# Delta rule with feature-major outputs: sums of squares by VectorE's 32x32 turns

## The chip, the cores and the metric

The kernel runs on one core of a Trainium2 chip. The metric is the device time of one execution in microseconds. A core has five engines that work through queues of their own and wait for each other by semaphores: TensorE (PE, with its weight loads as PEld), VectorE (DVE), ScalarE (ACT), GpSimd (POOL), and SyncE (SP), which here only issues DMAs. DMAs are also issued from POOL's queue.

## What is computed

A decoder of two layers over 1,024 tokens of 1,024 features. Each layer projects the normed input once, feeds a sparse attention branch and a gated delta rule branch, gates both, adds them and projects the sum back:

```python
for layer in range(DEPTH):
    h = rms_norm(x, norm_gain[layer])
    proj = h @ w_in[layer]
    ...
    y_a = dsa_attention(q_a, k_a, v_a, q_i, k_i, w_i) * jax.nn.silu(z_a)
    qkv_b = jax.nn.silu(causal_depthwise_conv(qkv_b, conv_w[layer]))
    ...
    q_b = l2_normalize(q_b.reshape(B, S, GDN_HEADS, GDN_DK))
    k_b = l2_normalize(k_b.reshape(B, S, GDN_HEADS, GDN_DK))
    ...
    o_b = chunked_gated_delta_rule(q_b, k_b, v_b, beta, g).astype(x.dtype)
    y_b = (rms_norm(o_b, gdn_norm_gain[layer]) * jax.nn.silu(z_b)).reshape(B, S, GDN_WIDTH)
    gates = jax.nn.sigmoid(gate_l).reshape(B, S, N_BRANCH, D_MODEL)
    mixed = gates[:, :, 0, :] * y_a + gates[:, :, 1, :] * y_b
    x = x + mixed @ w_out[layer]
return rms_norm(x, final_gain)
```

The change concerns two normalizations of the delta rule branch, which has eight heads of 128 features: the length of each token's query (`l2_normalize(q_b)`) and the mean square of each token's output (`rms_norm(o_b)`). The delta rule is linear in the query. So the kernel runs it on raw queries and divides once, at the output: with the sum of squares of a raw query Q, and of an unnormalized output O over 128 features, the factor for a token is the inverse root of O/128 + 128 EPS (Q + 4 EPS), apart from constants.

## The kernel before

**Phases.** Each layer has a token phase (index scores and top-k selection beside token-major projections), a feature phase (the delta rule and the remaining gates) and an attention phase with the output projection. The change lies in the feature phase, which runs from about 340 us to 1,000 us in layer 0 and once more from about 1,600 us in layer 1.

**The feature phase.** `feature_phase` goes over the eight heads. For each it projects keys, queries and values (`kf`, `qf`, `vv`, each with 128 features on the partitions and 1,024 tokens in the free dimension) and then two gates of the head before. A projection half is 24 matmuls of 512 columns (L419): eight blocks of 128 input features, three products each, because every f32 operand is split into a high and a low part (`w_hi`, `w_lo`; the split is a cast on ACT, L164, and a subtraction on DVE, L165). A head is 6 halves for kf, qf and vv and 4 for the gates, 240 matmuls in all.

**The order of the work.** All else is hung onto these matmuls. `self.count` counts them, and `plan_head` writes for each step of a head the count at which it is issued (`AT_...`, relative to the head's start; the first head's late steps are 28 later). After each matmul, `planned` issues the steps that are due, with a high priority, and a list scheduler then orders each engine's instructions by what it reckons to be ready. A head's steps spread over more than two of its own lengths of 240, so a stretch of 240 counts holds the late steps of one head, the chunks of the next and the early steps of a third. Below, a count within such a stretch is the count since its kf projection began.

**A head's steps**, in their order:
- `conv` (L847): three DVE passes over 1,024 columns (L866), a tanh on ACT into the buffer `xp` (L868), a last DVE pass (L869).
- `decays_load` (L824): SP loads 512 KB of decay rows into `H`, each row of DRAM read for all 128 partitions (L831); POOL masks it (L832) and then issues the load of `qe`, 512 KB of the same kind (L838).
- `gdn_keys` (100, 106): four PE transposes per half, squares on ACT, a reduce (L885) and the scaled copy `kdec` on DVE (L897), then some ten DVE steps on 8 columns for the keys' lengths (`g_rk` to `g_nce`).
- `gdn_queries` (142, 147): four PE transposes of `qf` per half (L878), squares on ACT (L884), a reduce on DVE (L885); then `zq` (L931).
- `gdn_row` (152): sends the row of key factors through DRAM, `cscr` (L919) to `g_ccomp` (L922), and with `gdn_products` (151 to 163) come the key-key and query-key products. `A` holds the decayed query-key products.
- `gdn_inverse`, `inverse_pairs` (336 to 366, so 96 to 126 of a later stretch): the inverse of a triangular matrix per chunk of 128 tokens. In 32x32 blocks it goes through DRAM and a chain of small DVE steps (L1050, L1052); the pairs are then joined on PE. DVE turns blocks into `xf` (L1069), PE makes L1078, L1085, L1092, then L1098, from which DVE makes `xf` (L1100), which PE uses in L1104.
- `gdn_chunks` (374 on, one step each 7 counts): for eight chunks in turn, the state `st`, the update `u`, and the output `po`. Its products put tokens on the partitions (L996, L997). ACT copies `po` into `vb` and squares it with an accumulated sum per token into `osq` (L998, L1000).
- `gdn_finish` (L1004): the gates of the head (`gate` tiles, 128x512, features on the partitions), then `norms` (537): `ms` from `osq` and `zq`, the inverse root in eleven small DVE steps (`rsqrt`, L147 to L160), the scaling of `vb` (L1015); and `outputs` (546, 552): four PE transposes of `vb` per half (L1021), a product with gain and gate from PSUM on DVE (L1022), a store to `yb` (L1023).

Of the kernel before, what the change touches and what calls it, by code (L numbers as in the profile page):

```python
# [20 lines left out]
try:  # L21
# [4 lines left out]
F32 = mybir.dt.float32  # L26
# [5 lines left out]
OP = mybir.AluOpType  # L32
# [4 lines left out]
P = 128  # L37
# [42 lines left out]
    76, (126, 130, 134, 138), (100, 106), (142, 147), (151, 155, 159, 163), 152, 184, (204, 210))  # L80
AT_SECOND, AT_PAIRS, AT_CHUNKS, AT_NORMS, AT_OUTPUTS = 38, 336, 374, 537, (546, 552)

STEP_PAIRS, STEP_CHUNKS = 6, 7
# [24 lines left out]
class Trunk:  # L108
    def __init__(self, ctx, tc, args):
        self.tc, self.nc = tc, tc.nc  # L110
        (self.x, self.positions, self.norm_gain, self.w_in, self.conv_w, self.a_log, self.dt_bias,
         self.gdn_gain, self.idx_gain, self.w_out, self.final_gain, self.out) = args
        self.depth = self.w_in.shape[0]
        self.const = ctx.enter_context(tc.tile_pool(name="const", bufs=1))
        self.dram = ctx.enter_context(tc.tile_pool(name="scratch", bufs=1, space=DRAM))
        self.small = ctx.enter_context(tc.tile_pool(name="small", bufs=2))
        edge = ctx.enter_context(tc.tile_pool(name="edge", bufs=1)).tile([P, 32], F32, name="edge")
        self.nc.vector.memset(edge, 0.0)
        self.act = ctx.enter_context(tc.tile_pool(name="act", bufs=1))
        self.wp = ctx.enter_context(tc.tile_pool(name="bulk", bufs=1))  # L120
        self.tags, self.turn = {}, 0
        self.beside, self.credit = None, 0.0
        self.ahead, self.scored = {}, False
        self.plan, self.count, self.act_last = [], 0, None
        ctx.enter_context(self.banks(acc=(1, 2), tr=(1, 2)))
# [20 lines left out]

    def rsqrt(self, v, n, y=None):  # L147

        nc = self.nc
        if y is None:  # L150
            y = self.small.tile([P, n], F32, name="rs_y")
        t = self.small.tile([P, n], F32, name="rs_t")
        yi = y.bitcast(I32)
# [27 lines left out]
    def constants(self, first):  # L181
# [25 lines left out]
        for q in range(4):  # L207
            nc.gpsimd.affine_select(self.xinit[32 * q:32 * q + 32], self.xinit[32 * q:32 * q + 32],
                                    pattern=[[4, 8], [-1, 32]], compare_op=OP.not_equal, fill=1.0, base=q,
                                    channel_multiplier=0)  # L210
        self.rope_tables()

        self.feat, self.ig, self.nexpa, self.dtb = [], [], [], []
# [518 lines left out]

    def gated(self, l, ht, cz, cg, tag="acc"):

# [3 lines left out]
        for half in range(2):  # L738
            b = p.tile([P, 512], F32, name="gate", bufs=2)
            for i in range(2):  # L740
# [7 lines left out]

    def gate_a(self, l, ht, f, tag="acc", then=None):

        for _ in self.gate_steps(l, ht, f, tag, then):
            pass

    def gate_steps(self, l, ht, f, tag, then=None):
        for half, b in enumerate(self.gated(l, ht, C_ZA + f * P, C_GA + f * P, tag)):
            self.stored = self.nc.sync.dma_start(out=self.ya[f, :, 512 * half:512 * half + 512], in_=b).ins
# [5 lines left out]
    def feature_phase(self, l, ht):  # L762
# [6 lines left out]
        with tc.tile_pool(name="early", bufs=1) as pe, tc.tile_pool(name="decays", bufs=1) as pd, \  # L769
# [10 lines left out]
            for h in range(HEADS + 1):  # L780
                before, hd = hd, None
                if h < HEADS:
                    hd = dict(h=h, at=self.count)
                    self.plan_head(p, hd, XF)
                    for name, base, bufs in (("kf", 1024, 3), ("qf", 0, 3), ("vv", 2048, 1)):
                        self.conv(l, pe if name == "vv" else p, ht, hd, name, base, bufs)
                if h in GATED:
                    i = 1 + GATED.index(h)
                    for f in range(sum(GATES[:i]), sum(GATES[:i + 1])):
                        self.gate_a(l, ht, f)  # L790
                if before:
# [3 lines left out]
    def plan_head(self, p, hd, XF):  # L795
# [21 lines left out]
        chunks = self.gdn_chunks(p, hd)  # L817
        at(AT_CHUNKS, *[lambda: next(chunks, None)] * (3 * T - 1), gap=STEP_CHUNKS)

    def zeros(self, a):  # L820
# [26 lines left out]
    def conv(self, l, p, ht, hd, name, base, bufs):  # L847
# [22 lines left out]
        if name == "kf":  # L870
            self.behind = done.ins

    def turned(self, src, half):
# [50 lines left out]
    def gdn_queries(self, hd, half):  # L924

        self.squares(self.turned(hd["qf"], half), hd["ssq"][:, 8 + 4 * half:12 + 4 * half])
        if half == 1:


            zq = hd["zq"] = self.small.tile([P, T], F32, name="g_zq")  # L930
            self.nc.vector.tensor_scalar(zq, hd["ssq"][:, 8:16], 4 * EPS, P * EPS, op0=OP.add, op1=OP.mult)  # L931

    def gdn_products(self, p, hd, c):
# [30 lines left out]
    def gdn_chunks(self, p, hd):  # L964
# [3 lines left out]
        egt = self.egt[:, :, h]  # L968
        osq = hd["osq"] = sm.tile([P, T], F32, name="g_osq")
        st = None  # L970
        for c in range(T):
# [14 lines left out]
            if c < T - 1:  # L986
# [5 lines left out]
                else:  # L992
                    nc.vector.scalar_tensor_tensor(new, st, egt[:, c:c + 1], pn, op0=OP.mult, op1=OP.add)
            po = self.bank("oc")[:, :P]
            if st is not None:
                nc.tensor.matmul(po, qf[:, cs], st, start=True, stop=False)  # L996
            nc.tensor.matmul(po, A[:, c], u, start=st is None, stop=True)  # L997
            nc.scalar.copy(vb[:, c], po)  # L998
            junk = self.pl.tile([P, P], F32, name="o_junk", bufs=1)
            nc.scalar.activation(junk, po, AF.Square, accum_out=osq[:, c:c + 1])  # L1000
            st = new
            yield

    def gdn_finish(self, l, p, ht, hd):  # L1004
# [12 lines left out]
        def outputs(half):  # L1017
# [5 lines left out]
            nc.sync.dma_start(out=self.yb[h, :, 512 * half:512 * half + 512], in_=b)  # L1023

        self.at(hd["at"] + AT_NORMS, norms)
        for half in range(2):
# [365 lines left out]
```

## Time and profile before

| | |
|---|---|
| median of 3 runs | 2548.41 us (2547.25 to 2548.49) |
| profiled execution | 2547.07 us, its span 2545.3 us |
| PE busy | 2508.8 us, 99% |
| PEld busy | 2100.8 us, 83% |
| DVE busy | 1875.3 us, 74% |
| ACT busy | 1329.9 us, 52% |
| POOL busy | 207.4 us, 8% |
| granted TensorE clock | 0.995 |
| DMA | 211.35 MB, mean 83 GB/s |

An instruction's row gives its start in us from the span's start, its duration, engine, line, operation, and the tiles written and read (out<-in). Brackets hold the idle time of the engine before it and what ended that. A group's row gives the count, the busy time in us, the mean duration in ns, and idle time before the group's instructions. Matmuls overlap: a record of 0.39 us can be followed by the next after 0.23. What a matmul costs PE is therefore read from the spacing of starts. POOL's and SP's rows of DMAs tell when one is issued, not when it lands.

### The profile page before, as it was taken

To read this page: it belongs to the slowest core of one execution; us is meant where nothing else is said; L and a number is where in the kernel's file an instruction comes from. 1 tells how busy PE (TensorE), PEld (TensorE's weight loads), DVE (VectorE), ACT (ScalarE), POOL (GpSimd) and SP (SyncE) were. 2 spreads that over 40 slices of the span, in tenths; PEclk is the share of its full clock that TensorE was granted. 3 is DMA by queue.
4 is the path that set the end of the run, shared out by engine and by line. 5 is a ranking of instruction groups with operands and counts; after the bars stand their busy time and mean duration, and the time that the engine had idled before them with its cause. 6 is when DMAs were issued, how large, how long until landed. Compare 5 with 4: busy or idle time off the path is not lost.

```text
span 2545.3 us, 42024 instructions
## 1 busy us (share of the span) xinstructions
PE 2508.8 (99%) x14874; PEld 2100.8 (83%) x14874; DVE 1875.3 (74%) x5057; ACT 1329.9 (52%) x3052; POOL 207.4 (8%) x510
## 2 busy tenths in 40 slices
PE   8999999999999999999999999999999999999998
PEld 7778878888888888898897788788888888888986
DVE  7569997777787773797555789877777787638965
ACT  5449943344444342797234598334344444338952
POOL 0234000000000000000202330000000000000010
PEclk9999999999999999999999999999999999999999
DMA  4123243322333331431421232433322222324223
GB/s 129 55 67 102 66 103 77 73 53 70 69 70 75 75 92 60 156 95 33 157 74 52 73 97 71 100 72 71 76 52 68 72 73 69 103 86 133 82 94 126
DMA packets 290807, 211.35 MB, mean 83 GB/s; under 512 B 72290, under 2 KB 252356, under 8 KB 290596
## 3 DMA queue, kind: packets, MB, share of 16 engines
q1 hardware_dynamic: 277876, 167.43, 24.4%
q0 software_dynamic: 12576, 40.97, 5.5%
q8 instruction: 117, 1.92, 0.3%
q14 instruction: 94, 0.77, 0.1%
q10 hardware_dynamic: 144, 0.26, 0.0%
HBM read 162.19 MB, written 46.40 MB: 82 GB/s over the span
## 4 chain that ended last, share of the span: by engine, by line
PE 64%; DVE 20%; issue 7%; ACT 3%; DMA 3%; POOL 2%; SPq 0%; DVEq 0%; ACTq 0%; POOLq 0%
PE acc L419 20%; PE more L419 9%; PE acc L394 8%; PE acc L1257 4%; PE wide L1225 4%; DVE xtmp L1050 3%; DVE t_junk L646 3%; DVE xc L1052 3%; PE tr L1248 2%; PE tr L944 2%; PE out L394 2%; DVE w_lo L165 2%; DVE kf L866 2%; PE tr L878 2%; DMA w_raw<-in_w_in_dram 1%
## 5 line engine op out<-in xcount | busy, mean ns | idle before, releaser
L419 PE MATMUL acc<-hi_t,w_hi 128*128 128x512 f32 x1152 | 468.9, 407 | 7.1 <-ACT th L743 7.1
L419 PE MATMUL acc<-lo_t,w_hi 128*128 128x512 f32 x1152 | 467.2, 406 | 0.0
L419 PE MATMUL acc<-hi_t,w_lo 128*128 128x512 f32 x1152 | 463.4, 402 | 0.0
L164 ACT CAST w_hi<-w_raw 128x512 fp32r<-128x512 f32 (+1 forms) x336 | 200.3, 604 | 301.5 <-PE acc L419 134.3
L165 DVE TENSOR_TENSOR w_lo<-w_raw,w_hi 128x512 fp32r<-128x512 f32 (+1 forms) x336 | 222.5, 670 | 130.2 <-ACT w_hi L164 112.4
L394 PE MATMUL acc<-w_hi,hi_t 128*128 128x512 f32 (+1 forms) x688 | 254.4, 370 | 8.6 <-ACT hi_t L164 7.9
L419 PEld LDWEIGHTS acc<-hi_t,w_hi 128*128 128x128 f32 x1152 | 218.6, 190 | 46.6 <-ACT th L743 7.9
L419 PEld LDWEIGHTS acc<-hi_t,w_lo 128*128 128x128 f32 x1152 | 218.7, 190 | 39.9
L394 PE MATMUL acc<-w_lo,hi_t 128*128 128x512 f32 (+1 forms) x688 | 250.3, 364 | 0.0
L419 PEld LDWEIGHTS acc<-lo_t,w_hi 128*128 128x128 f32 x1152 | 218.7, 190 | 37.6
L394 PE MATMUL acc<-w_hi,lo_t 128*128 128x512 f32 (+1 forms) x688 | 249.6, 363 | 0.0
L664 ACT ACTIVATE t_sign<-scores,t_bits 128x640 f16<-128x640 f32 x248 | 196.4, 797 | 7.9 <-DVE t_bits L656 4.1
L419 PE MATMUL more<-hi_t,w_hi 128*128 128x512 f32 x480 | 194.5, 405 | 0.0
L419 PE MATMUL more<-lo_t,w_hi 128*128 128x512 f32 x480 | 194.3, 405 | 0.0
L419 PE MATMUL more<-hi_t,w_lo 128*128 128x512 f32 x480 | 192.6, 401 | 0.0
L394 PEld LDWEIGHTS acc<-w_hi,hi_t 128*128 128x128 f32 x688 | 129.7, 188 | 33.5 <-ACT hi_t L164 8.2
L394 PEld LDWEIGHTS acc<-w_hi,lo_t 128*128 128x128 f32 x688 | 129.8, 189 | 18.9 <-issue 0.5
L646 DVE TENSOR_SCALAR_CACHE_REDUCE t_junk<-scores,t_bits 128x768 f16<-128x768 f32 x124 | 142.1, 1146 | 4.2
L394 PEld LDWEIGHTS acc<-w_lo,hi_t 128*128 128x128 f32 x688 | 129.7, 188 | 17.4 <-issue 0.5
L620 DVE SCALAR_TENSOR_TENSOR scores<-relu,w_idx,scores 128x384 f32<-128x384 f32 (+5 forms) x84 | 80.5, 959 | 57.1 <-ACT relu L612 49.0
L1050 DVE TENSOR_TENSOR xtmp<-wide,xc 128x60 f32<-128x60 f32 (+24 forms) x496 | 106.1, 214 | 14.2
L1052 DVE TENSOR_TENSOR xc<-xc,xtmp 128x60 f32<-128x60 f32 (+24 forms) x496 | 104.4, 211 | 14.0
(388 smaller groups left out, 5742.9 us busy)
## 6 DMA issues: line engine op xcount, KB each, us to landing
w_raw<-in_w_in_dram SPq DMA_DIRECT2D x272, 256.0 KB
qs<-stage POOLq DMA_DIRECT2D x32, 256.0 KB, 2.3
ya_gate<-gate SPq DMA_DIRECT2D x32, 256.0 KB
H<-rows SPq DMA_DIRECT2D x16, 512.0 KB
wide<-hscr SPq DMA_DIRECT2D x64, 128.0 KB
yb<-gate SPq DMA_DIRECT2D x32, 256.0 KB
qraw<-qs SPq DMA_DIRECT2D x32, 256.0 KB
w_raw<-in_w_out_dram SPq DMA_DIRECT2D x32, 256.0 KB
```

The lines of the kernel that those rows point to most:

```text
L164: self.nc.scalar.copy(hi, src)
L165: self.nc.vector.tensor_sub(lo, src, hi.bitcast(F32))
L394: mm = nc.tensor.matmul(acc[t][:, :n], a[:, k, ts], ws[k][b][:, :n], start=k == 0 and i == 0, stop=k == KT - 1 and i == 2)
L419: mm = self.nc.tensor.matmul(acc, ws[k // 4][a][:, cs], act[b][:, k, hs], start=k == 0 and i == 0, stop=k == KT - 1 and i == 2)
L620: nc.vector.scalar_tensor_tensor(sc[:, :n], rel[half][:, u], wc, sc[:, :n], op0=OP.mult, op1=OP.add)
L646: nc.vector.tensor_scalar(junk[:, :sc[i].shape[1]], sc[i], thr, 0.0, op0=op, op1=OP.add, accum_out=cnt[:, i:i + 1])
L664: nc.scalar.activation(junk[:, :n], sc[i], AF.Sign, bias=f(bits, i), scale=-1.0, accum_out=cnt[:, i:i + 1])
L866: nc.vector.scalar_tensor_tensor(dst, xp[:, 1 + j:1 + j + S], cw(j), dst, op0=OP.mult, op1=OP.add)
L1050: nc.vector.tensor_mul(tmp[:, :n, j + 1:], ln[:, None, j, j + 1:].to_broadcast(shape), X[:, :n, j:j + 1].to_broadcast(shape))
L1052: nc.vector.tensor_add(X[:, :n, j + 1:], X[:, :n, j + 1:], tmp[:, :n, j + 1:])
L1225: nc.tensor.matmul(ps[:, :w], qt[a][:, i], kt[b][:, g, o:o + w], start=j == 0, stop=j == 2)
L1257: nc.tensor.matmul(po, a, b[:, cs], start=j == 0 and i == 0, stop=j == t and i == 2)
```

## The change

Seven of the eight heads of each layer, all but the last, get a new path (`flat`):

- In `gdn_chunks` the operands of the output products change places, so `po` comes with features on the partitions and tokens in the free dimension. ACT copies it into `vb` and writes its square, without a sum, over the used `A`.
- Sums over features now run across partitions. `gdn_sums` (458 for half 0, 537 for half 1): DVE turns each 32x32 block of the squares (into `kdec`, no longer needed), then reduces over groups of 32 columns. That leaves in `ro`, for each of 32 token groups, sums over a quarter of the features. `gdn_queries` makes the same of the queries: a DVE turn of `qf` into `xp`, one square of 1,024 columns on ACT, one DVE reduce into `rq`. One step adds both.
- `gdn_roots` (550): one PE product of `ro` with `quads`, a constant of 32 columns, adds the quarters; `ms`, the same eleven steps of the inverse root on 32 partitions and 32 columns; SP stores the 1,024 factors as 4 KB (`roots`) and loads them for all 128 partitions, 512 KB, over `A`.
- `gains` (541, 545): DVE multiplies `vb`, gain and gate from SBUF. `scaled` (604, 608): DVE multiplies that by the factors in `A`, and SP stores `yb`.
- The last gates of the phase (`gate_a` at the end) write into a `kf` tile, since the `gate` tiles are held longer. The constant `quads` is made at the start by four DVE steps from the identity, in place of a memset.

```diff
+AT_SUMS, AT_ROOTS, AT_GAINS, AT_SCALED = (458, 537), 550, (541, 545), (604, 608)
...
-        edge = ctx.enter_context(tc.tile_pool(name="edge", bufs=1)).tile([P, 32], F32, name="edge")
-        self.nc.vector.memset(edge, 0.0)
+        self.quads = ctx.enter_context(tc.tile_pool(name="edge", bufs=1)).tile([P, 32], F32, name="edge")
...
+        nc.vector.tensor_add(self.quads, self.ident[:, 0:32], self.ident[:, 32:64])
+        for q in (2, 3):
+            nc.vector.tensor_add(self.quads, self.quads, self.ident[:, 32 * q:32 * q + 32])
+        nc.vector.tensor_scalar(self.quads, self.quads, 1.0 / P, None, op0=OP.mult)
...
-                    hd = dict(h=h, at=self.count)
+                    hd = dict(h=h, at=self.count, flat=h < HEADS - 1)
...
-                        self.gate_a(l, ht, f)
+                        dst = None if h < HEADS else p.tile([P, S], F32, name="kf", bufs=3)
+                        self.gate_a(l, ht, f, dst=dst)
...
+        if hd["flat"]:
+            for half in range(2):
+                at(AT_SUMS[half], lambda half=half: self.gdn_sums(hd, half))
...
     def gdn_queries(self, hd, half):
 
+        if hd["flat"]:
+            nc, xq = self.nc, hd["xq"][:, 4:]
+            if half == 0:
+                nc.vector.transpose(xq, hd["qf"])
+                nc.scalar.activation(xq, xq, AF.Square)
+            else:
+                hd["rq"] = self.pl.tile([P, 32], F32, name="rq", bufs=2)
+                nc.vector.tensor_reduce(hd["rq"], xq.rearrange("p (b d) -> p b d", d=32), axis=AX.X, op=OP.add)
+            return
...
+    def gdn_sums(self, hd, half):
+
+        nc = self.nc
+        a, b = (hd[k].rearrange("p c i -> p (c i)")[:, 512 * half:512 * half + 512] for k in ("A", "kdec"))
+        if half == 0:
+            hd["ro"] = self.pl.tile([P, 32], F32, name="ro", bufs=2)
+        ro = hd["ro"]
+        nc.vector.transpose(b, a)
+        nc.vector.tensor_reduce(ro[:, 16 * half:16 * half + 16], b.rearrange("p (b d) -> p b d", d=32), axis=AX.X,
+                                op=OP.add)
+        if half == 1:
+            nc.vector.scalar_tensor_tensor(ro, hd["rq"], P * P * EPS, ro, op0=OP.mult, op1=OP.add)
+
+    def gdn_roots(self, hd):
+
+        nc = self.nc
+        pt = self.tr()[:32, :32]
+        nc.tensor.matmul(pt, hd["ro"], self.quads, start=True, stop=True)
+        ms = self.pl.tile([P, 32], F32, name="ms", bufs=1)[:32]
+        nc.vector.tensor_scalar(ms, pt, 4 * EPS * P * EPS, None, op0=OP.add)
+        rs = self.rsqrt(ms, 32, rows=32)
+        row = self.dram.tile([32, 32], F32, name="roots", bufs=2)
+        nc.sync.dma_start(out=row, in_=rs)
+        nc.sync.dma_start(out=hd["A"].rearrange("p c i -> p (c i)"), in_=ap(row, 0, [[0, P], [1, S]]))
...
+            turn = (lambda a, b: (b, a)) if flat else (lambda a, b: (a, b))
             if st is not None:
-                nc.tensor.matmul(po, qf[:, cs], st, start=True, stop=False)
-            nc.tensor.matmul(po, A[:, c], u, start=st is None, stop=True)
+                nc.tensor.matmul(po, *turn(qf[:, cs], st), start=True, stop=False)
+            nc.tensor.matmul(po, *turn(A[:, c], u), start=st is None, stop=True)
             nc.scalar.copy(vb[:, c], po)
-            junk = self.pl.tile([P, P], F32, name="o_junk", bufs=1)
-            nc.scalar.activation(junk, po, AF.Square, accum_out=osq[:, c:c + 1])
+            if flat:
+                nc.scalar.activation(A[:, c], po, AF.Square)
...
+        def flat(name, half):
+            return hd[name].rearrange("p c i -> p (c i)")[:, 512 * half:512 * half + 512]
+
+        def gains(half):
+            b = gates[half]
+            self.behind = nc.vector.scalar_tensor_tensor(b, flat("vb", half), feat[:, 96:97], b, op0=OP.mult,
+                                                         op1=OP.mult).ins
+
+        def scaled(half):
+            b = gates[half]
+            nc.vector.tensor_mul(b, b, flat("A", half))
+            nc.sync.dma_start(out=self.yb[hd["h"], :, 512 * half:512 * half + 512], in_=b)
+
+        if hd["flat"]:
+            self.at(hd["at"] + AT_ROOTS, lambda: self.gdn_roots(hd))
+            for half in range(2):
+                self.at(hd["at"] + AT_GAINS[half], lambda half=half: gains(half))
+                self.at(hd["at"] + AT_SCALED[half], lambda half=half: scaled(half))
+            return
```

The scheduler moves other instructions as well. Line numbers of the changed program are higher (L866 becomes L874, L1100 becomes L1169). The places shown are those of the head whose stretch runs from 711.4 to 787.2 us in the trace before, the sixth of layer 0.

DVE, from the end of the triangular chain on, where the head two before finishes. Before, between the three passes of the key convolution (`kf`), stand the first steps of the outputs' norm (`g_ms`, `rs_y`):

```order
L866 SCALAR_TENSOR_TENSOR kf<-xp_3861,feat_755,kf 128x1024
L1013 SCALAR_TENSOR_TENSOR g_ms<-g_osq,g_zq 128x8
L866 SCALAR_TENSOR_TENSOR kf<-xp_3861,feat_755,kf 128x1024
L154 TENSOR_SCALAR rs_y<-g_ms 128x8
L866 SCALAR_TENSOR_TENSOR kf<-xp_3861,feat_755,kf 128x1024
L155 TENSOR_SCALAR rs_y<-rs_y 128x8
L157 TENSOR_TENSOR rs_t<-rs_y 128x8
```

Now, in the changed program, the same place holds half 1's turn, one gain, the reduce, the sum `ro`, and `ms`, which waits for PE's product:

```order
L874 SCALAR_TENSOR_TENSOR kf<-xp_3864,feat_758,kf 128x1024
L959 STREAM_TRANSPOSE kdec<-A 128x512
L1080 SCALAR_TENSOR_TENSOR gate<-vb,feat_758,gate 128x512
L960 TENSOR_REDUCE ro<-kdec 128x16
L874 SCALAR_TENSOR_TENSOR kf<-xp_3864,feat_758,kf 128x1024
L963 SCALAR_TENSOR_TENSOR ro<-rq,ro 128x32
L874 SCALAR_TENSOR_TENSOR kf<-xp_3864,feat_758,kf 128x1024
L971 TENSOR_SCALAR ms<-tr 32x32
L1138 STREAM_TRANSPOSE xf<-H 32x8x32
L154 TENSOR_SCALAR rs_y<-ms 32x32
```

The other gain of the head (half 0) stands earlier, beside half 0's turn and reduce. On PE the eight transposes of `vb` stood after count 88 of the stretch; the product with `quads` stands after count 73, and L1104 has moved from 128 to 129.

DVE again, in the second key and query part of the stretch: `g_v` and `g_rk` are the key norms' steps, `qf` the query convolution, `xf` the operand of PE's L1104. Before:

```order
L903 TENSOR_SCALAR g_v<-g_ssq 128x8
L1080 TENSOR_TENSOR y_8025<-ch,g_nc 32x256
L154 TENSOR_SCALAR g_rk<-g_v 128x8
L866 SCALAR_TENSOR_TENSOR qf<-xp_3862,feat_755,qf 128x1024
L155 TENSOR_SCALAR g_rk<-g_rk 128x8
L866 SCALAR_TENSOR_TENSOR qf<-xp_3862,feat_755,qf 128x1024
L157 TENSOR_TENSOR rs_t<-g_rk 128x8
L1100 TENSOR_TENSOR xf<-ch,g_nc 64x512
```

Now:

```order
L913 TENSOR_SCALAR g_v<-g_ssq 128x8
L1149 TENSOR_TENSOR y_7926<-ch,g_nc 32x256
L154 TENSOR_SCALAR g_rk<-g_v 128x8
L1085 TENSOR_TENSOR gate<-gate,A 128x512
L155 TENSOR_SCALAR g_rk<-g_rk 128x8
L1085 TENSOR_TENSOR gate<-gate,A 128x512
L157 TENSOR_TENSOR rs_t<-g_rk 128x8
L874 SCALAR_TENSOR_TENSOR qf<-xp_3865,feat_758,qf 128x1024
L158 SCALAR_TENSOR_TENSOR rs_t<-rs_t,g_v 128x8
L1169 TENSOR_TENSOR xf<-ch,g_nc 64x512
```

Both scaled multiplications (L1085) stand ahead of `xf`, and one pass of `qf` has gone behind it.

SP's queue from the load of the next decay rows (`H`) on. Before:

```order
L831 DMA H<-rows 128x8x128
L356 DMA w_raw<-in_w_in_dram 128x4x128
L1023 DMA yb<-gate 128x512 x2
L356 DMA w_raw<-in_w_in_dram 128x4x128 x2
L919 DMA cscr<-g_crow 8x128
L922 DMA g_ccomp<-cscr 32x32 x4
```

Now:

```order
L839 DMA H<-rows 128x8x128
L360 DMA w_raw<-in_w_in_dram 128x4x128
L974 DMA roots<-rs_y 32x32
L360 DMA w_raw<-in_w_in_dram 128x4x128
L975 DMA A<-roots 128x1024
L1086 DMA yb<-gate 128x512 x2
L360 DMA w_raw<-in_w_in_dram 128x4x128 x2
L929 DMA cscr<-g_crow 8x128
L932 DMA g_ccomp<-cscr 32x32 x4
```

The write and the load of the roots stand behind `H` and a weight tile; the stores of `yb`, two weight tiles and `cscr` stand behind the load.

More of the change, by code (lines that the diff above doesn't have):

```diff
@@ L145, in tr, with rsqrt @@
         return self.bank("tr")
-    def rsqrt(self, v, n, y=None):
+    def rsqrt(self, v, n, y=None, rows=P):
         nc = self.nc
         if y is None:
-            y = self.small.tile([P, n], F32, name="rs_y")
-        t = self.small.tile([P, n], F32, name="rs_t")
+            y = self.small.tile([P, n], F32, name="rs_y")[:rows]
+        t = self.small.tile([P, n], F32, name="rs_t")[:rows]
         yi = y.bitcast(I32)
@@ L730, in select, with gated @@
             yield SEL_COST
-    def gated(self, l, ht, cz, cg, tag="acc"):
+    def gated(self, l, ht, cz, cg, tag="acc", dst=None):
         nc = self.nc
@@ L738, in gated @@
         for half in range(2):
-            b = p.tile([P, 512], F32, name="gate", bufs=2)
+            b = p.tile([P, 512], F32, name="gate", bufs=2) if dst is None else dst[:, 512 * half:512 * half + 512]
             for i in range(2):
@@ L747, in gated, with gate_a, gate_steps @@
             yield b
-    def gate_a(self, l, ht, f, tag="acc", then=None):
-        for _ in self.gate_steps(l, ht, f, tag, then):
-            pass
-    def gate_steps(self, l, ht, f, tag, then=None):
-        for half, b in enumerate(self.gated(l, ht, C_ZA + f * P, C_GA + f * P, tag)):
+    def gate_a(self, l, ht, f, tag="acc", then=None, dst=None):
+        for _ in self.gate_steps(l, ht, f, tag, then, dst):
+            pass
+    def gate_steps(self, l, ht, f, tag, then=None, dst=None):
+        for half, b in enumerate(self.gated(l, ht, C_ZA + f * P, C_GA + f * P, tag, dst)):
             self.stored = self.nc.sync.dma_start(out=self.ya[f, :, 512 * half:512 * half + 512], in_=b).ins
@@ L871, in conv @@
             self.behind = done.ins
+        elif name == "qf":
+            hd["xq"] = xp
     def turned(self, src, half):
@@ L968, in gdn_chunks @@
         egt = self.egt[:, :, h]
-        osq = hd["osq"] = sm.tile([P, T], F32, name="g_osq")
+        flat = hd["flat"]
+        osq = None if flat else sm.tile([P, T], F32, name="g_osq")
+        hd["osq"] = osq
         st = None
@@ L994, in gdn_chunks @@
             po = self.bank("oc")[:, :P]
+            turn = (lambda a, b: (b, a)) if flat else (lambda a, b: (a, b))
             if st is not None:
-                nc.tensor.matmul(po, qf[:, cs], st, start=True, stop=False)
-            nc.tensor.matmul(po, A[:, c], u, start=st is None, stop=True)
+                nc.tensor.matmul(po, *turn(qf[:, cs], st), start=True, stop=False)
+            nc.tensor.matmul(po, *turn(A[:, c], u), start=st is None, stop=True)
             nc.scalar.copy(vb[:, c], po)
-            junk = self.pl.tile([P, P], F32, name="o_junk", bufs=1)
-            nc.scalar.activation(junk, po, AF.Square, accum_out=osq[:, c:c + 1])
+            if flat:
+                nc.scalar.activation(A[:, c], po, AF.Square)
+            else:
+                junk = self.pl.tile([P, P], F32, name="o_junk", bufs=1)
+                nc.scalar.activation(junk, po, AF.Square, accum_out=osq[:, c:c + 1])
             st = new
```

## The prediction

> **What bounds the kernel now.** I read the busy shares of the page first, then the table by windows over whole heads of the feature phase, then the groups of the instructions that go, then the timelines of all engines around the places where something new waits. Of the page, one line:
>
> ```profile
> PE 2508.8 (99%) x14874; PEld 2100.8 (83%) x14874; DVE 1875.3 (74%) x5057; ACT 1329.9 (52%) x3052; POOL 207.4 (8%) x510
> ```
>
> TensorE (PE) is never idle for long, so time leaves the kernel only with PE work, or comes in as PE waits. The windows of two whole heads of layer 0 (columns: length, busy time and count of PE, PEld, DVE, ACT, POOL; clock; DMA):
>
> ```profile
> 635.60:711.40 75.80, 75.67 (x492) 63.16 (x492) 58.16 (x158) 32.40 (x87) 1.94 (x2) 1.00 0.30 69
> 711.40:787.20 75.80, 75.66 (x492) 63.15 (x491) 58.14 (x157) 32.37 (x87) 2.03 (x2) 1.00 0.30 69
> ```
>
> A head lasts 75.8 us; PE is idle for 0.14 us of it, at full clock. VectorE (DVE) has 17.7 us to spare in a head, ScalarE (ACT) 43. So the question is what a head loses on PE, and whether the new DVE and DMA work makes PE wait.
>
> **PE work that goes.** Two groups, and the timeline where four such transposes stand between projection matmuls:
>
> ```profile
> L878 PE MATMUL tr<-ident,qf 128*128 128x128 f32 x128 | 20.7, 276 | 0.7 <-DVE qf L869 0.5
> L1021 PE MATMUL tr<-ident,vb 128*128 128x128 f32 x128 | 17.7, 279 | 3.3 <-DVE vb L1015 2.0
> ...
> 770.72 0.39 PE L419 MATMUL acc<-hi_t,w_lo 128*128 128x512 f32 x1
> 770.95 0.60 PE L878 MATMUL tr<-ident,vv 128*128 128x128 f32 x4
> 771.30 0.48 PE L419 MATMUL acc<-hi_t,w_hi 128*128 128x512 f32 x1
> 771.63 0.27 PE L977 MATMUL ch<-g_s,kf 128*128 128x128 f32 x1
> ```
>
> From 770.72 to 771.63 there are 0.91 us; two projection matmuls at their spacing of 0.23 take 0.46, so four transposes cost 0.45 us of stream, 0.113 each. The recorded 276 ns overlap with the neighbours. Sixteen go per head: 1.81 us, and 25.3 us over the 14 heads that take the new path. The idle time before L1021 goes too: 3.3 us in 16 heads, 0.2 a head.
>
> [...]
>
> What comes in on PE is one 32-column product with quads per head. No row has it: a projection matmul of 512 columns, 0.23 us, bounds it above, a sixteenth of the L1104 group below (742.85 less 741.78, 0.07 us) from the other side. I take 0.1. The turned operands of the two output products change neither their number nor their size.
>
> **DVE work.** The groups that give prices:
>
> ```profile
> L885 DVE TENSOR_REDUCE g_ssq<-th 128x4 f32<-128x512 f32 x64 | 43.4, 681 | 17.9 <-ACT th L884 17.9
> L744 DVE SCALAR_TENSOR_TENSOR gate<-th,gate 128x512 f32<-128x512 f32 x64 | 44.0, 687 | 32.2 <-ACT th L743 32.0
> L1022 DVE SCALAR_TENSOR_TENSOR gate<-tr,feat,gate 128x512 f32<-128x512 f32 x32 | 22.7, 747 | 3.8 <-PE tr L1021 2.3
> L1069 DVE STREAM_TRANSPOSE xf<-H 32x256 f32<-32x256 f32 x48 | 20.7, 432 | 2.1 <-DMA H<-xscr 1.1
> L1015 DVE TENSOR_TENSOR vb<-vb,rs_y 128x1024 f32<-128x1024 f32 x16 | 19.6, 1224 | 0.5
> L158 DVE SCALAR_TENSOR_TENSOR rs_t<-rs_t,g_ms 128x8 f32<-128x8 f32 x48 | 8.0, 167 | 1.6
> ```
>
> Out, per head: two reduces of the queries (1.36), zq, ms and eleven steps of the square root (13 x 0.167 = 2.17), the scaling of vb (1.22), two L1022 (1.49): 6.2 us. In: turns of 1,024 and twice 512 columns, reduces of the same sizes (1.36 + 1.36), gains and scaled (4 x 0.687 = 2.75), and 13 small steps on 32 columns at about 0.2 (2.6). A turn of these sizes is not in the trace: L1069 says 1.69 us for 1,024 if it scales by columns, an ordinary pass (L1015) 1.22; I take 1.22 and 0.69, as for any other pass of that size, and keep the rest for the range. Sum 10.7 us, up to 11.5. So DVE has 4.5 to 5.3 us a head more to do, against 17.7 idle. As a sum it is covered; what counts is where it stands.
>
> **The new chain.** Per head, half 1's sums, the roots product, the root, a 4 KB write, a 512 KB broadcast load into A, and two multiplications that wait for it. Its places in the head from 711.4 on, by the timelines of DVE, then SP and POOL:
>
> ```profile
> 719.09 1.29 DVE L866 SCALAR_TENSOR_TENSOR kf<-xp,feat,kf 128x1024 f32<-128x1024 f32 x1 [0.38 <-ACT kf L860]
> 720.29 0.16 DVE L1013 SCALAR_TENSOR_TENSOR g_ms<-g_osq,g_zq 128x8 f32<-128x8 f32 x1
> ...
> 739.84 0.69 DVE L1100 TENSOR_TENSOR xf<-ch,g_nc 64x512 f32<-64x512 f32 x1 [0.26 <-PE ch L1098]
> ...
> 745.12 1.23 DVE L869 SCALAR_TENSOR_TENSOR qf<-xp,qf 128x1024 f32<-128x1024 f32 x1 [2.29 <-ACT xp L868]
> ...
> 748.19 0.69 DVE L885 TENSOR_REDUCE g_ssq<-th 128x4 f32<-128x512 f32 x1 [0.93 <-ACT th L884]
> ...
> 759.83 0.68 DVE L744 SCALAR_TENSOR_TENSOR gate<-th,more 128x512 f32<-128x512 f32 x1
> ```
>
> ```profile
> 723.95 0.45 SPq L831 DMA_DIRECT2D H<-rows  x1
> 731.37 0.38 SPq L356 DMA_DIRECT2D w_raw<-in_w_in_dram  x1
> 746.97 0.38 SPq L356 DMA_DIRECT2D w_raw<-in_w_in_dram  x1
> ...
> 751.77 0.31 SPq L919 DMA_DIRECT2D cscr<-g_crow  x1
> 753.79 1.73 SPq L922 DMA_DIRECT2D g_ccomp<-cscr  x4
> ...
> 732.77 1.18 POOL L832 TENSOR_SCALAR_AFFINE_SELECT H<-H 128x1024 f32<-128x1024 f32 x1 [73.36 <-DMA yb<-gate]
> 733.90 0.90 POOL L838 DMA_DIRECT2D qe<-rows  x1
> ```
>
> and of PE:
>
> ```profile
> 726.48 0.39 PE L419 MATMUL more<-hi_t,w_lo 128*128 128x512 f32 x1
> 726.71 0.39 PE L419 MATMUL more<-hi_t,w_hi 128*128 128x512 f32 x1
> 727.24 1.09 PE L1021 MATMUL tr<-ident,vb 128*128 128x128 f32 x8
> 728.09 0.47 PE L419 MATMUL more<-lo_t,w_hi 128*128 128x512 f32 x1
> 728.40 0.39 PE L419 MATMUL more<-hi_t,w_lo 128*128 128x512 f32 x1
> ...
> 738.66 1.14 PE L1098 MATMUL ch<-xf,H 64*64 64x64 f32 x16
> ...
> 741.46 0.39 PE L419 MATMUL acc<-lo_t,w_hi 128*128 128x512 f32 x1
> 741.78 1.14 PE L1104 MATMUL ch<-H,xf 64*64 64x64 f32 x16
> 742.85 0.50 PE L419 MATMUL acc<-hi_t,w_lo 128*128 128x512 f32 x1
> ```
>
> On DVE a successor starts about 0.08 us before the recorded end (719.09 + 1.29 against 720.29). With the new order: kf from 719.09, turn, gain, reduce, kf, ro: 1.20 + 3 x 0.61 + 1.20 + 0.20, ro is there at 723.4. PE came to count 88 at 726.94; the product now stands at count 73, so 15 x 0.23 earlier, 723.5. Wait there: 0 to 0.4, I take 0.1. Then kf, ms, three turns of xf at 0.45, eleven small steps at 0.22, the second kf line, one w_lo: 1.2 + 0.2 + 1.35 + 2.4 + 1.14 + 0.61, the root is done at 730.4. SP writes it; cscr to g_ccomp shows write and turnaround, 2.0 us, so the load into A goes out at 732.4.
>
> How long that load takes, no row says. The nearest rows:
>
> ```profile
> 13.80 0.43 SPq L1321 DMA_DIRECT2D x<-in_x_dram  x1
> ...
> 17.56 1.06 ACT L300 ACTIVATE sq_junk<-x 128x1024 f32<-128x1024 f32 x1 [1.27 <-DMA x<-in_x_dram]
> ...
> qe<-rows POOLq DMA_DIRECT2D x14, 512.0 KB, 7.6
> ```
>
> Same size and same 4 KB rows, read once each: 3.8 us. Rows read 128 times over, in 512-byte pieces: 7.6, and for H from 723.95 until POOL may start at 732.77. A is read in 4 KB rows, but 128 times over, behind H and two weight tiles in one queue, with qe in flight from 733.9. I take the middle, 5.6: A lands at 738.0; the bounds are 736.2 and 740.0.
>
> DVE comes to the first scaled multiplication at 735.8 (after 730.4: w_lo 0.61, qf 1.2, two reduces and two kdec at 0.6, two y at 0.4, two small), so it waits 2.2 us. Queued behind it are scaled, steps of the key norms, a qf line and L1100, whose xf PE's L1104 needs: 2 x 0.61 + 3 x 0.2 + 1.2, then 0.69. So xf is there 3.7 us after A lands: 741.7. PE wants it at 741.78, less 1.23 (1.69 from 726.71 to 728.40 without two matmuls: transposes and wait), plus 0.1 and one count more, 0.23: 740.9. **PE waits 0.8 us in each head;** 0 with A at 736.2, 2.8 at 740.0. Later in the head DVE recovers in the 2.29 us before L869.
>
> **Edits with no cost.** ACT loses two squares and eight accumulator reads per head for one square of 1,024 columns and is 57% idle. In SP's queue two yb stores, two weight tiles and cscr stand behind A's load; the weight tile after the next could not go out before 746.97, which covers 8 us; without the cover a late w_lo would delay a projection. The gate tile is held some 10 us longer; its next write, at 759.83, is 20 us away. Four 128x32 steps and an x load moved back at the start: -1 to +3 us, taken as 0, since PE starts on what ACT finishes there.
>
> **Sum.** Per head -1.81 - 0.2 + 0.1 + 0.1 + 0.8 = -1.0 us; 14 heads -14.1. The profiled execution took 2547.07 us (span 2545.3 and 1.8 around it), so 2533.0; the median of the three runs, 2548.41, lies 1.3 above the profiled one: 2534.3, say 2534.5. A measurement can tell about 0.2%, 5 us, from no change.
>
> **Rivals.**
> *All of the gain stays.* A lands by 736.2, or DVE reaches it later than I think. Then -1.8 a head, -25.4: 2523. For it: x's 3.8 us. Against: the crowded queue. Chance 0.25.
>
> *Slower: A shares the engines with qe.* POOL's load goes out at 733.9 and is under way until 741.5 (7.6); if A's packets take turns with it, A lands at 740.0 or later, PE waits 2.8 us at L1104, the head is 1.0 us longer, the kernel +14: 2562.5. It is slower from the point at which A lands after 739.0. For it: the overlap is certain if A goes out at 732.4. Against: A's longer pieces. Chance 0.15.
>
> [...]
>
> *No change.* DVE's extra 5 us fall into its full stretches (queries beside vv and the products, 748 to 760) and PE waits for products and g_r as well, another 1.0 us a head: 2548. For it: 1.2 us more in a stretch without a gap. Against: the 2.29 us idle before it. Chance 0.13.
>
> The forecast has 0.45; 0.02 remains for what I don't see. Range 2521 to 2557: it leaves out most of the slower case and little below the full gain. Faster 0.70, same 0.13, slower 0.17.
>
> **What would show it.** Right: heads of about 74.8 us; DVE idle some 2 us before scaled on the load of A, then PE idle before L1104's successor. Full gain: heads of 74.0, no idle time there. Slower: heads above 76 with that wait near 3 us. Wrong in the PE term: heads that differ though PE waits nowhere.

## The result, and the profile after

The changed kernel takes 2560.97 us in the median of 14 runs (2546.74 to 2570.38); the kernel before took 2548.05 in 14 runs beside them (2545.81 to 2548.55). The ratio is 1.0051, 95% interval 1.0032 to 1.0069: slower by half a per cent, where 2534.5 was forecast. The single runs spread over 24 us, those of before over 3. The profiled execution is the slowest of the 14: 2570.38 us, span 2568.6.

The page after, the line of busy times:

```profile
PE 2503.0 (97%) x14678; PEld 2092.1 (81%) x14678; DVE 1924.7 (75%) x5130; ACT 1321.8 (51%) x2926; POOL 208.6 (8%) x510
```

PE's busy time fell by 5.8 us only, and its idle time rose from 36.5 (2545.3 less 2508.8) to 65.6 us. The windows over the heads of layer 0, second stretch to sixth (columns as in the prediction):

```profile
407.40:488.30 80.90, 78.40 (x450) 64.63 (x449) 57.98 (x154) 29.87 (x70) 0.00 (x0) 0.89 0.25 53
488.30:569.80 81.50, 78.59 (x490) 64.84 (x489) 63.45 (x173) 32.65 (x82) 2.04 (x2) 0.96 0.32 70
569.80:653.40 83.60, 76.09 (x478) 63.35 (x477) 62.70 (x165) 31.95 (x79) 1.94 (x2) 0.96 0.34 69
653.40:727.40 74.00, 74.00 (x478) 61.61 (x477) 61.66 (x163) 31.83 (x78) 1.94 (x2) 1.00 0.34 77
727.40:801.50 74.10, 74.06 (x479) 61.64 (x478) 61.63 (x163) 31.88 (x79) 1.94 (x2) 1.00 0.36 78
```

Two kinds of heads stand here. Some last 74.0 us, PE never idle: the 1.8 us are gained in full. Others last 80 to 84 us, with PE idle and its clock below 1. The waits, PE's first and then DVE's for the factors (columns: us in total, times, longest):

```profile
PE ch L1173 <- issue: 23.8, 6, 7.5
PE ch L1147 <- DVE xf L1138: 4.0, 2, 2.2
PE ch L1167 <- ACT xf L1162: 3.1, 2, 2.9
PE tr L988 <- DVE H L991: 2.0, 1, 2.0
...
DVE gate L1085 <- DMA A<-roots: 38.0, 11, 8.8
```

The first row is the wait that the prediction put at 0.8 us in every head: here it is 1.8 to 7.5 us in five heads and at most 0.3 in the others. What tells the heads apart shows in their timelines. A long head, the stretch from 569.8:

```profile
582.81 0.45 SPq L839 DMA_DIRECT2D H<-rows  x1
588.23 0.34 SPq L974 DMA_DIRECT2D roots<-rs_y  x1
592.25 1.08 POOL L840 TENSOR_SCALAR_AFFINE_SELECT H<-H 128x1024 f32<-128x1024 f32 x1 [71.45 <-DMA w_raw<-in_w_in_dram]
593.29 0.90 POOL L846 DMA_DIRECT2D qe<-rows  x1
594.33 0.34 SPq L975 DMA_DIRECT2D A<-roots  x1
603.58 0.69 DVE L1085 TENSOR_TENSOR gate<-gate,A 128x512 f32<-128x512 f32 x1 [8.76 <-DMA A<-roots]
606.33 0.69 DVE L1169 TENSOR_TENSOR xf<-ch,g_nc 64x512 f32<-64x512 f32 x1
607.13 1.93 PE L1173 MATMUL ch<-H,xf 64*64 64x64 f32 x16 [7.51 <-issue]
```

And the next one, a short head:

```profile
665.71 0.45 SPq L839 DMA_DIRECT2D H<-rows  x1
671.82 0.33 SPq L974 DMA_DIRECT2D roots<-rs_y  x1
674.74 1.08 POOL L840 TENSOR_SCALAR_AFFINE_SELECT H<-H 128x1024 f32<-128x1024 f32 x1 [80.56 <-DMA w_raw<-in_w_in_dram]
675.67 0.34 SPq L975 DMA_DIRECT2D A<-roots  x1
675.78 0.90 POOL L846 DMA_DIRECT2D qe<-rows  x1
679.25 0.69 DVE L1085 TENSOR_TENSOR gate<-gate,A 128x512 f32<-128x512 f32 x1 [1.11 <-DMA A<-roots]
683.13 1.14 PE L1173 MATMUL ch<-H,xf 64*64 64x64 f32 x16
```

In the short head A's load goes out 0.11 us ahead of qe and has landed 3.6 us after its issue. In the long one it goes out 1.04 us behind qe and takes 9.25; DVE stands for 8.8 us at L1085, `xf` (L1169) is behind it in DVE's order, and PE runs dry. Over the heads of this trace: A ahead of qe by 0.1 to 0.8 us, or no qe at all, 3.5 to 3.9 us from issue to the first multiplication; A behind by 0.06, 5.7; by 0.41, 0.43 and 0.43, 3.9, 8.3 and 7.6; by 0.9 to 1.04, 9.25, 9.3 and 10.2. (The first changed head of each layer is apart: there DVE comes late or qe is through.) The packet records show why A can be late though its issue is only 0.43 us behind (the heads of 8.3 and 7.6 us). A's packets begin 1 us after its issue, and still 1.3 and 1.55 us ahead of qe's. In the 3 us from the first, 116 and 123 of its 128 packets start, but the last ones run among qe's, until 7.2 and 7.0 us after the issue. In the long head shown, 96 of qe's 128 packets have started before A's first.

In layer 0 both loads are let go by the same landing, that of `H`: qe follows POOL's mask, and the 4 KB store of the roots, which must land before A can go out, comes through just after `H`. There A's load goes out 3.85 to 6.1 us after the store; in the last changed head of the layer, with no `H` under way, 1.4 us after it. In layer 1 the store goes out about when `H` lands and is not held up: A follows it after 1.9 to 2.7 us, against 2.2 with no `H`. In both layers A's load goes out 0.8 to 2.1 us after POOL starts on `H`, and qe's 1.0 to 1.9 us after. So the two issues fall within about a microsecond of each other, and which is first changes from head to head in this trace. That it changes from run to run as well is an estimate, from the 24 us over which the single runs spread.

Last, the clock. Windows after the gap at 607 and after one of 2.2 us at 434.6 (the column before the last two):

```profile
430.00:435.00 5.00, 2.50 (x25) 1.76 (x25) 3.20 (x9) 3.17 (x10) 0.00 (x0) 0.92 0.67 98
435.00:440.00 5.00, 5.00 (x63) 3.79 (x60) 4.67 (x16) 1.98 (x4) 0.00 (x0) 0.50 0.48 62
450.00:455.00 5.00, 5.00 (x39) 4.33 (x39) 3.59 (x7) 0.83 (x2) 0.00 (x0) 0.87 0.02 2
...
605.00:610.00 5.00, 2.87 (x18) 2.60 (x19) 4.66 (x15) 0.90 (x3) 0.00 (x0) 0.50 0.30 108
```

These two gaps cost more than themselves: the granted clock fell to 0.50, by the trace's clock records for 17.1 us from 434.2 on and for 6.8 us from 604.9 on. In the heads of this trace 54.6 us run at half clock. The whole time adds up: 29.1 us more idle, less the 5.8 by which PE's busy time fell, are 23.3, the difference of the spans. If the 25.3 us of PE work that the prediction counted are gone, half clock has put back an estimated 19.5 of them.

### The profile page after: what moved, and what is told of

It reads as the page before. It is cut to its first block, busy times and chain, and to the rows that moved or that the text cites. A ratio compares the mean times of both kernels' runs of the same rounds, so it can differ in the third digit from the quotient of the medians.

```text
span 2568.6 us, 41728 instructions
## 1 busy us (share of the span) xinstructions
PE 2503.0 (97%) x14678; PEld 2092.1 (81%) x14678; DVE 1924.7 (75%) x5130; ACT 1321.8 (51%) x2926; POOL 208.6 (8%) x510
## 3 DMA queue, kind: packets, MB, share of 16 engines
q1 hardware_dynamic: 280564, 174.83, 25.3%
## 4 chain that ended last, share of the span: by engine, by line
PE 67%; DVE 12%; issue 10%; POOL 5%; DMA 4%; ACT 2%; SPq 0%; POOLq 0%; DVEq 0%; ACTq 0%
PE acc L423 24%; PE more L423 11%; PE acc L398 6%; PE acc L1326 4%; PE wide L1294 4%; PE tr L1317 2%; DVE t_junk L650 2%; PE tr L988 2%; PE out L398 2%; DMA w_raw<-in_w_in_dram 2%; PE ch L1028 1%; PE oc L1044 1%; PE tr L888 1%; PE ch L1034 1%; DVE w_lo L165 1%
## 5 line engine op out<-in xcount | busy, mean ns | idle before, releaser
L1045 ACT COPY vb<-oc 128x128 f32<-128x128 f32 x128 | 34.0, 265 | 163.5 <-PE oc L1044 160.9
L1121 DVE TENSOR_TENSOR xc<-xc,xtmp 128x60 f32<-128x60 f32 (+24 forms) x496 | 104.4, 211 | 14.4
```

The costliest lines, as they stand in the source:

```text
L1121: nc.vector.tensor_add(X[:, :n, j + 1:], X[:, :n, j + 1:], tmp[:, :n, j + 1:])
```

## The experiments

Three theories. **Order:** A's landing hangs on whether its packets are out before qe's; a late A stops DVE, then PE, then halves the clock. **Load:** DVE's extra work (3.5 us a head by the pages) is what costs. **Broadcast:** 512 KB read 128 times over takes that long by itself, whatever qe does. Each kernel ran beside the kernel before; ratios are to that.

**1. The multiplications later.**

```diff
+            with self.tc.issue_after(self.queried):
                 nc.vector.tensor_mul(b, b, flat("A", half))
```

`queried` is the query turn (L939) of the head two later. The counts of the multiplications also move, from (604, 608) to (624, 628), here and in 7 to 9.

> Edit: both multiplications by the roots (scaled) are put behind the query turn of the head two later, some 9 us further on in VectorE's order; nothing else is asked for. Order theory (the load of A lands in 3.5 to 4 us when its packets are out before those of qe and in 8 to 10 us when qe is first; VectorE then stands still before scaled, TensorE runs out of work behind it and its clock falls to half): even a late A is there by then, the waits of TensorE between the two 64x64 product groups go in all heads, and the median comes to about 2536 us (2528 to 2544), with only the early gaps of each layer left. Load theory (VectorE's 4.5 us more per head are what costs): nothing is taken from VectorE, so 2555 to 2565. Broadcast theory (A's 512 KB take long by themselves, whatever qe does): as the order theory, this run does not tell those two apart.

Measured: 2543.61 us (2534.39 to 2549.15), ratio 0.9986 (0.9976 to 0.9996). In experiment 1, a head where qe was first by 1.1 us, and the sixth changed head, whose successor by two has no query turn, so that scaled kept its early place:

```profile
587.09 0.34 SPq L975 DMA_DIRECT2D A<-roots  x1
...
598.95 1.25 DVE L1085 TENSOR_TENSOR gate<-gate,A 128x512 f32<-128x512 f32 x2
...
892.79 0.69 DVE L1085 TENSOR_TENSOR gate<-gate,A 128x512 f32<-128x512 f32 x1 [8.98 <-DMA A<-roots]
```

No wait in the first, 8.98 us in the second, and there alone a gap at L1173, of 7.6 us. With all of DVE's work in place the kernel lost 17 us: the load theory does not account for that. The time came out 7.6 us above the 2536 expected, with that one gap left and 10.2 us of half clock behind it.

**2. qe behind A, by the order of the program.**

```diff
-        with self.tc.issue_after(prior):
+        with self.tc.issue_after(prior), self.tc.issue_after(self.rooted or prior):
             queue.dma_start(out=qe...
```

> Edit: GpSimd's load of qe waits for the landing of A's load of the head two before; the order of instructions on all engines is unchanged. Order theory: A's packets never meet qe's, A lands 3.5 to 4.5 us after its issue in all heads, TensorE's waits behind scaled go, the median comes to about 2536 us (2528 to 2544); qe lands some 9 us before it is used. Broadcast theory: A still lands late in about half the heads, the time stays at 2555 to 2565. Load theory: 2555 to 2565 as well, with A early.

Measured: 2561.42 us (2553.36 to 2563.44), ratio 1.0045 (1.0033 to 1.0057), as the changed kernel. It decides nothing: the edit (`rooted` is A's load) orders instructions for the scheduler and put no wait into the program; qe still went out first by 1.0 us in the same head of layer 0 (591.7 against 592.7).

**3. The multiplications on GpSimd.**

```diff
-            nc.vector.tensor_mul(b, b, flat("A", half))
+            nc.gpsimd.tensor_mul(b, b, flat("A", half))
```

> Edit: GpSimd does the two multiplications by the roots in place of VectorE, behind its load of qe. Order theory: a late A holds up GpSimd alone, which has nothing due; no gap of TensorE between the two 64x64 product groups, and 1.4 us a head less on VectorE: about 2534 us (2524 to 2544). Load theory: a third of VectorE's 4.5 us goes, so a third of the loss of 13 us plus the gain: 2550 to 2558. A rival of its own: GpSimd's multiplications slow VectorE's down or take so long that the tile of A is freed too late for the products: then above 2550, with waits of VectorE on GpSimd.

Measured: 2540.18 us (2536.63 to 2545.21), ratio 0.9971 (0.9963 to 0.998). The waits of experiment 3:

```profile
DVE A L990 <- POOL gate L1085: 3.9, 1, 3.9
...
PE ch L1173 <- ACT H L853: 1.8, 2, 1.1
```

At L1173 1.8 us are left of 23.8. Once DVE waits 3.9 us for POOL to give the tile of A free: the rival's mishap, in one head. The gaps of the early heads stay (2.2, 3.2, 1.8 and 3.1 us). DVE's busy time did not fall, 1925.7 us against 1924.7, though 28 multiplications, some 19 us, have left it: its other instructions took longer by nearly as much, and the kernel still gained 20.8 us.

**4. The first head of each layer by the old path.**

```diff
-                    hd = dict(h=h, at=self.count, flat=h < HEADS - 1)
+                    hd = dict(h=h, at=self.count, flat=0 < h < HEADS - 1)
```

> Edit: the first head of each layer takes the old path as well as the last, so six heads a layer are changed in place of seven. Order theory plus a part of its own for the starts: the gaps at the second and third head of a layer (2.2, 2.9, 1.8 and 2.0 us, with 10.8 us of half clock in the profiled run) come from the triangular chain, which takes 23.6 us there in place of 18.0 because the new sums and gains stand in it; they go, two heads' gain of 1.8 us goes with them, and the race with qe stays in the other heads: about 2546 us (2536 to 2556) and still a spread of 15 us or more from run to run. Load theory: a seventh of the loss goes, 2557 to 2561.

Measured: 2555.87 us (2543.4 to 2568.82), ratio 1.0029 (1.0013 to 1.0046). The waits of experiment 4:

```profile
PE ch L1173 <- issue: 17.9, 3, 7.3
...
PE ch L1147 <- DVE xf L1138: 1.3, 2, 0.7
```

The early gaps are gone, those of the late A are there, and so is a spread of 25 us. The median is at the upper end of what was expected.

**5. qe behind A, by a wait.**

```diff
+        prior = prior if self.rooted is None else nc.gpsimd.tensor_copy(
+            qe[0:1, 0:1], self.rooted[0:1, 0, 0:1]).ins
```

Here `rooted` is the tile A that is being loaded.

> Edit: GpSimd copies one element of the landed A into qe just ahead of its load of qe, so that this load cannot go out before A of the head two before is there; it holds for five heads of each layer, not for the first changed head. What the run before it (qe behind A by order alone) was to show, now with a wait in the program. Order theory: in these heads A lands 3.5 to 4.5 us after its issue, VectorE waits under 2 us for it, no gap of TensorE behind scaled; the gaps of the early heads stay; 2538 us (2532 to 2546). Broadcast theory: A still takes 8 to 10 us in about half the heads, 2555 to 2565. Load theory: A early, TensorE waits all the same, 2555 to 2565.

Measured: 2538.97 us (2534.84 to 2545.09), ratio 0.9964 (0.9953 to 0.9976). The head in which A had been late by 9.25 us, in experiment 5:

```profile
588.68 0.34 SPq L975 DMA_DIRECT2D A<-roots  x1
592.48 0.69 DVE L1085 TENSOR_TENSOR gate<-gate,A 128x512 f32<-128x512 f32 x1 [3.36 <-DMA A<-roots]
592.62 0.59 POOL L844 COPY qe<-A 1x1 f32<-1x1 f32 x1 [4.93 <-DMA A<-roots]
593.51 0.90 POOL L846 DMA_DIRECT2D qe<-rows  x1 [0.30 <-POOL qe L844]
```

Landed after 3.8 us. In the five heads of layer 0 with this wait A takes 3.5 to 3.8 us, in all ten at most 4.7. The broadcast theory falls and the order theory stands: the same load, behind the same `H`, is early when qe is held, and nothing was taken from DVE. The experiment shows that qe makes A late. It does not show that the first packet decides, and in experiment 7 one load whose packets began 1.1 us ahead of qe's was through only 8.8 us after its issue. What is left in this head, 3.36 us on DVE and 1.8 on PE, is the store of the roots, 5.9 us behind `H`.

**6 and 7. Both causes taken away**, with the multiplications on GpSimd (6), or late on DVE in all heads (7); the first head of each layer takes the old path in both. 6 is the edits of 3 and 4 together; 7 those of 1 and 4, and

```diff
-        self.squares(self.turned(hd["qf"], half), hd["ssq"][:, 8 + 4 * half:12 + 4 * half])
+        self.queried = self.squares(self.turned(hd["qf"], half), hd["ssq"][:, 8 + 4 * half:12 + 4 * half])
```

so that the sixth changed head has something to stand behind.

> Edit: both of the edits that helped, the multiplications by the roots on GpSimd and the first head of each layer by the old path. Order theory with the early heads as a second cause of their own: no gap of TensorE over 1.5 us is left in the heads, the clock stays full, and twelve heads keep 1.8 us each: 2548 less 21.6 and some for the start, 2524 to 2530. If the two causes overlapped (one gap feeding the other), the gains would not add: 2535 to 2540. Load theory: 2540 or more.

> Edit: the multiplications stay on VectorE, behind the query work of the head two later in all heads, and the first head of each layer takes the old path. Order theory: VectorE comes to scaled some 9 us later than in the changed kernel, so a late A costs nothing or nearly: 2524 to 2534, with 1.4 us more on VectorE than the version on GpSimd. Load theory: VectorE's 4.5 us more are all still there, 2545 to 2560.

Measured: 2530.48 us (2525.29 to 2533.32), ratio 0.9922 (0.9908 to 0.9936), and 2524.76 us (2523.6 to 2526.91), ratio 0.9906 (0.9892 to 0.992). The gains do not eat each other: 30.5 us against 20.8 (3) plus 5.1 (4), and 36.2 against 17.4 (1) plus 5.1, where 7 also frees the sixth head. The time of 6 lies just above the 2524 to 2530 expected. In 7 no PE wait at L1173 is left, though qe was still first in some heads; in 6 gaps of 0.6 to 1.1 us are.

**8. The first head new again, its sums 45 places later.** From 7:

```diff
-                at(AT_SUMS[half], lambda half=half: self.gdn_sums(hd, half))
+                at(AT_SUMS[half] + (45 if hd["h"] + half == 0 else 0), lambda half=half: self.gdn_sums(hd, half))
```

> Edit: as the version with the multiplications late, but the first head of each layer takes the new path again, with its first half of the sums 45 places later, so that the turn, the reduce and the gain no longer stand in the second triangular chain. It parts the two gaps of the starts. If the sums in the chain make the gap of 2.9 to 3.4 us in the third stretch and the query work (turn and reduce in the first head) makes the gap of 2.2 us in the second: the chain is back at 17.5 to 18 us, the gap at the third stretch is gone, the one at the second stays, with its half clock: 2524.8 less 3.6 for two more heads, plus 3.9 us of gaps and 2 to 12 of clock, 2527 to 2537. If the sums make both: no gap is left, 2520 to 2523. If the chain is not what holds the third stretch up: both stay, 2535 to 2545.

Measured: 2540.1 us (2534.45 to 2542.06), ratio 0.9967 (0.9955 to 0.998). Another miss: the later place did not move the sums in DVE's order, the chain still took 23.6 us, and both gaps stayed. It only shows that the first heads cost 15 us against 7 when they take the new path.

**9. The first head's sums bound behind the chain.** From 8:

```diff
-        nc.vector.transpose(b, a)
+        with self.tc.issue_after(self.chained if hd["h"] == 0 else self.act_last):
+            nc.vector.transpose(b, a)
```

The same stands around the gains; `chained` is the last step of the chain (L1121).

> Edit: the run before this one left VectorE's order in the second triangular chain as it was, so it parted nothing. Here the turn, reduce and gains of the first changed head are bound to stand behind the last step of that chain, by the order of the program; the multiplications are late in all heads as before. If the sums and the gain in the chain make the gap of about 3 us in the third stretch of each layer: the chain takes 17.5 to 18.5 us in place of 23.6, this gap and its half clock go, the gap of 2.2 us in the second stretch stays: 2540 less 6 to 9, 2530 to 2535. If the sums make both gaps: 2520 to 2524. If the third stretch is held up by something else: the chain is shorter and the gap stays, 2538 to 2542.

Measured: 2523.66 us (2522.58 to 2524.09), ratio 0.9902 (0.9885 to 0.9918), the lowest median, though not told apart from 7 by the intervals. First and last sum of the second triangular chain on DVE and what stands in it, in the changed kernel:

```profile
477.72 0.19 DVE L1121 TENSOR_TENSOR xc<-xc,xtmp 128x31 f32<-128x31 f32 x1
...
479.46 0.74 DVE L1080 SCALAR_TENSOR_TENSOR gate<-vb,feat,gate 128x512 f32<-128x512 f32 x1
480.12 0.70 DVE L959 STREAM_TRANSPOSE kdec<-A 128x512 f32<-128x512 f32 x1
480.86 0.69 DVE L960 TENSOR_REDUCE ro<-kdec 128x16 f32<-128x512 f32 x1
...
496.72 1.28 DVE L874 SCALAR_TENSOR_TENSOR kf<-xp,feat,kf 128x1024 f32<-128x1024 f32 x1
...
501.30 0.18 DVE L1121 TENSOR_TENSOR xc<-xc,xtmp 128x8 f32<-128x8 f32 x1
```

and in experiment 9, with its third stretch, a later one and its page:

```profile
470.88 0.19 DVE L1121 TENSOR_TENSOR xc<-xc,xtmp 128x31 f32<-128x31 f32 x1
...
488.50 0.17 DVE L1121 TENSOR_TENSOR xc<-xc,xtmp 128x8 f32<-128x8 f32 x1
488.60 0.70 DVE L959 STREAM_TRANSPOSE kdec<-A 128x512 f32<-128x512 f32 x1
```

```profile
481.50:557.50 76.00, 75.82 (x491) 62.70 (x490) 65.14 (x172) 32.63 (x83) 1.96 (x2) 1.00 0.36 76
631.50:705.60 74.10, 74.10 (x479) 61.65 (x478) 61.71 (x163) 31.78 (x79) 1.94 (x2) 1.00 0.36 77
```

```profile
PE 2483.3 (98%) x14678; PEld 2075.3 (82%) x14678; DVE 1923.5 (76%) x5130; ACT 1320.3 (52%) x2926; POOL 209.5 (8%) x510
```

The chain takes 17.6 us in place of 23.6. Gain, turn and reduce are 2.0 us of the difference; three passes of a key convolution (the first is the row at 496.72) are another 3.6, and in experiment 9 these come behind the chain's end as well, at 490.5. The third stretch takes 76.0 in place of 81.5, and its gap is gone; the gap of 2.2 us in the second stretch is still there, as the first of the three outcomes has it. The time is better than that outcome's 2530: in the profiled run the gap at 434.7 brought no half clock at all (the clock is 1.00 over the stretch from 407.6 to 481.5), where that of experiment 8 brought 13.7 us. That part was luck as far as the traces go: seven of them show after this gap anything from 0 to 17.1 us of half clock. DVE is as busy as in the changed kernel (1923.5 against 1924.7 us): the load theory is out. PE is busy for 25.5 us less than before, at nearly the same total of half clock (31.8 against 29.2 us).

## Why the prediction was wrong

**PE work that goes: right.** 1.81 us a head and 25.3 in all; heads of 74.0 in place of 75.8, and 25.5 us on the page of experiment 9. The rival in which all of the gain stays, 2523, is what experiment 9 measures: it needed a late A off DVE's path and the first head's sums out of the chain.

**DVE's durations: right.** The turns took 1,235 and 705 ns, as ordinary passes of their size; the additional load is 3.5 us a head, under the 4.5 given, and harmless as a sum.

**The chain up to A's issue: right within 1.4 us in one head, further off in others.** In the stretch from 727.4, shifted by 16.0 us, the root was stored at 729.8 (730.4 forecast), A went out at 733.8 (732.4), DVE came to scaled at 736.1 (735.8). But the store's turnaround, put at 2.0 us after `cscr` and `g_ccomp`, took 3.85 to 6.1 us in layer 0, behind `H`.

**The landing of A: the step that failed.** It said "I take the middle, 5.6: A lands at 738.0", with bounds of 736.2 and 740.0, and from that "PE waits 0.8 us in each head". The middle is hardly met: of the twelve loads apart from the first heads, six take 3.5 to 3.9 us, five 7.6 to 10.2 and one 5.7, by how A's packets lie to qe's. In the long head A landed 20.8 us after `H` was issued, which on the clock of the prediction is 744.7, past the upper bound. Of these 6.7 us too much, 3.1 are the late issue behind the store and 3.65 the load. A mean over two cases priced neither: no head shows a wait of 0.8. (Three small slips in the working change nothing: the middle of 3.8 and 7.6 is 5.7, `ro` comes to 723.5 by its own terms and not 723.4, and L1069's 432 ns for 256 columns scale to 1.73 us and not 1.69.)

**The slower rival named the place and the partner, qe, but priced it evenly:** 2.8 us in every head, as if packets took turns. Measured are heads at no cost and heads at 7.5. "The overlap is certain if A goes out at 732.4" stood in the text and was worth more than 0.15; what the prediction did not ask is what releases the two issues, in layer 0 one landing. No run shows such even turns. In the long head the trace's first packets of A start 5.0 us after the issue, when qe's have been moving for 4 us, against 1.0 us in the short head: A came behind qe more than in turn with it. In the two heads 0.43 us behind, the last 12 and 5 of A's 128 packets, those later than 3 us after the first, started between qe's, over 2.9 and 2.1 us.

**No term for the clock.** Of the 46.9 us between the spans of the changed kernel and experiment 9, 27 are idle time and 20 are longer busy time of PE, with 54.6 against 3.4 us of half clock in the heads. A price for a PE gap has to hold both in this kernel.

**"As a sum it is covered" failed at the starts.** The prediction read one head in the middle of a layer. Head 0's places are shifted by 28, so its turn, reduce and gain fall into the triangular chain of the second head; `H` goes out 7.6 us later in the third stretch than in the next (20.6 against 13.0 us from its start), and ACT and PE wait behind it. Experiment 9 shows this for the third stretch: with the sums behind the chain, `H` goes out 13.0 us from its start there too. The gap of the second stretch goes only with the first head's whole new path (4, 6, 7); whether its query turn and reduce make it wasn't parted.

**The no-change rival,** PE waiting at the products in each head, shows nowhere: the heads of 74.0 us have no idle time.

## What to carry to other kernels

Before a load is put on a path, look for what releases its issue and what else the same event releases: two transfers let go within about a microsecond of each other raced here, and from pass to pass PE waited between 0 and 7.5 us. Price each order by itself, and not their mean. Let the engine that must not stop come to the data later (9 us cost nothing here), and keep what others wait for ahead of the waiting instruction in its order. Read a change of order at the first and second pass of a loop as well as in its steady state.

## What the runs showed of the hardware

In the changed kernel's trace PE's gaps of 0.64 to 1.98 us (seven of them) brought no half clock; those of 2.39, 2.91, 3.98, 4.20, 5.06, 7.39 and 7.51 us brought 6.8 us of it each, that of 6.69 brought 10.2 and that of 2.19 brought 17.1. In the kernel before, gaps of 0.62 to 0.90 us brought none, and those of 3.24, 3.86 and 7.93 us brought 6.8 each. Length alone does not say what follows: the same gap of 2.19 us at the same place brought 17.1, 3.4, 13.7, 17.1, 3.4, 13.7 and 0 us of half clock in seven traces (the changed kernel, and experiments 1, 2, 3, 5, 8, 9), and gaps of 1.4 us brought 6.8 us in experiments 1 and 5. That adds to the spread of one kernel's times; the race alone can make it, as experiment 4, without the early gaps, spread over 25 us.
